# Head norms of a differential attention: repeating the inverse roots over all partitions through DRAM instead of by a copy and four transposes

## The chip, the cores and the metric

The kernel runs on one core of one Trainium2 chip. The core has five engines that work at the same time and meet through semaphores: TensorE (PE; its weight loads are shown apart as PEld), VectorE (DVE), ScalarE (ACT), GpSimd (POOL) and SyncE (SP). Sixteen DMA engines move data between DRAM and the on-chip memory SBUF; a transfer is issued by SyncE, ScalarE or GpSimd, each of which has its own queue and works through it in order. TensorE writes only to PSUM, a small memory of eight banks.

The metric is the time of one execution of the whole program on the device, in microseconds (us). Lower is better. A profile is taken in an execution of its own.

## The reference

One decoder layer over a sequence of 1024 positions with 1024 channels, all in float32: a token mixer with two branches (differential attention A with four heads, and a dilated window attention B with three groups of four heads), gates, an output projection, and then a gated MLP with a short convolution. The change concerns branch A alone:

```python
    oa = diff_attention(qa, ka, va, lam)              # (softmax1 - lam * softmax2) @ v, causal
    oa = rms_norm(oa, diff_head_g[l]) * (1.0 - lam_init)
    ya = oa.reshape(b, s, A_WIDTH) @ w_a_out[l]

def rms_norm(x, g):
    xf = x.astype(jnp.float32)
    y = xf * lax.rsqrt(jnp.mean(xf * xf, axis=-1, keepdims=True) + NORM_EPS)
    return (y * g.astype(jnp.float32)).astype(x.dtype)
```

Every position of every head has 128 output values. They are divided by the root of their mean square. This is the head norm: one inverse root for each position and head.

## The kernel before, in words

All products keep float32 accuracy by splitting each operand into a high and a low part (`split`, line 148) and adding three TensorE products (`mm3`, line 153). The program goes through stages: norms and values at the start, attention A, attention B, gates and output projections, then the MLP.

**Attention A.** Head after head (loop at line 915), the kernel works on eight query blocks of 128 positions in the order 6, 7, 4, 5, 2, 3, 0, 1 (`attend_a`, line 749). For a block it computes two score rows (lines 767 and 768, into one of two `s` PSUM banks), adds the mask and takes the maxima on VectorE (line 770), exponentiates on ScalarE (line 777), combines both softmaxes (line 784), transposes the result through a `pt` PSUM bank (`turned`, line 693; two `pt` banks) and multiplies by the values (`pv`, line 703). The output `osb` lies transposed: the 128 channels of the head on the partitions, 512 positions along the free dimension. Projections of the next head, of the first heads of attention B and of gates fill TensorE's time between the blocks (`proj_t`, line 235, with `rotated`, line 679, or `put_gate`, line 248, as evacuation; three `acc` PSUM banks). Their weights are loaded by SyncE (line 126) and split by ScalarE and VectorE (lines 149 and 146).

**The head norm.** `head_norm` (line 829) runs once for each half of 512 positions of each of the four heads, so eight times. ScalarE squares `osb` into a tile with the tag `hn` (line 832), which has one buffer. Then two steps are put off:

- `sums` (line 836): products with a column of ones, one for each block of 128 positions (line 840; the trace holds eight TensorE instructions for the four), add the squares over the 128 channels. The result has the positions of a block on the partitions, four columns for four blocks. `rsqrt` (line 159) makes the inverse root from them in twelve small VectorE instructions on 128x4 values (lines 166 to 179). Then a VectorE copy (line 843) repeats each of the four columns 128 times into `spread`, a 128x512 tile in the `hn` buffer.
- `norm` (line 845): four TensorE transposes (line 848) turn `spread` in blocks into a `pt` bank. Now every partition holds the inverse roots of all 512 positions along the free dimension. VectorE multiplies `osb` by this bank (line 849), and SyncE stores the result to `oa_d` in DRAM (line 850).

**What sets the order.** `later(n, fn)` (line 266) puts a step off by n query blocks: `sums` is due after one, `norm` after three. The steps that are due are called between the blocks, at a raised priority. From the instructions called in this way a planner makes each engine's queue: it simulates a timeline with costs of its own for every instruction and transfer, and issues what is ready by priority. So the order on an engine follows from the priorities and from when the planner expects an operand. Once written, a queue is worked through in order: an instruction that waits holds up everything behind it on its engine.

**GpSimd.** `side` (line 724) is `nc.gpsimd.dma_start`, a transfer issued by GpSimd. In the stretch of attention A its queue holds only the masks: `mask_a` before it (line 719), and `mask_b` for attention B at its end (lines 939 to 946), whose place in SBUF becomes free when an `osb` has been stored. In attention B `merge` (line 1042) uses the queue: it reads the statistics from `st_d` (line 1048), stores its weights to `e_d` (line 1071) and reads them back repeated on all partitions into `mw` (line 1077).

Of the kernel before, what the change touches and what calls it, by code (L numbers as in the profile page):

```python
# [15 lines left out]
F32 = mybir.dt.float32  # L16
# [3 lines left out]
ALU = mybir.AluOpType  # L20
# [4 lines left out]
P = 128  # L25
S = 1024
D = 1024
KC = D // P
AH, QK = 4, 64
# [58 lines left out]
def trunk(ctx: ExitStack, tc: tile.TileContext, a, out):  # L88
    nc = tc.nc
    dma = nc.sync.dma_start  # L90

    def open_pool(stack, name, bufs=1, side="left", **kw):
        if "space" not in kw:
            kw.update(side=side, reuse_waits="tile")
        return stack.enter_context(tc.tile_pool(name=name, bufs=bufs, **kw))
# [3 lines left out]
    cols, gpre, rstd = (edge[:, i * 8 : (i + 1) * 8] for i in range(3))  # L99
# [3 lines left out]
    dram = open_pool(ctx, "dram", space=DRAM)  # L103
    acc = open_pool(ctx, "acc", bufs=3, space=PSUM)
    pt = open_pool(ctx, "pt", bufs=2, space=PSUM)

    def psum(dt=F32, pool=acc, tag="acc"):
        return pool.tile([P, 512], dt, tag=tag, name=tag)
# [50 lines left out]
    def rsqrt(ss, n, pool, tag, eps=EPS):  # L159

        width = ss.shape[-1]
        v, y, w = (pool.tile([P, width], F32, tag=tag + c, name=tag + c) for c in "vyw")
        if isinstance(eps, float):
            nc.vector.tensor_scalar(v, ss, 1.0 / n, eps, op0=ALU.mult, op1=ALU.add)
        else:
            nc.vector.scalar_tensor_tensor(v, ss, 1.0 / n, eps, op0=ALU.mult, op1=ALU.add)
        nc.vector.tensor_scalar(y.bitcast(I32), v.bitcast(I32), -0.5, RSQRT_MAGIC, op0=ALU.mult, op1=ALU.add)

        f = 1.0
        for _ in range(3):  # L170
            if width == 1:
                nc.vector.tensor_scalar(w, y, y, v, op0=ALU.mult, op1=ALU.mult)
                nc.vector.tensor_scalar(y, w, -3.0 * f * f, y, op0=ALU.add, op1=ALU.mult)
            else:
                nc.vector.tensor_tensor(w, y, y, op=ALU.mult)
                nc.vector.tensor_tensor(w, w, v, op=ALU.mult)
                nc.vector.scalar_tensor_tensor(y, w, -3.0 * f * f, y, op0=ALU.add, op1=ALU.mult)
            f = -2.0 * f * f * f
        nc.vector.tensor_scalar(y, y, 1.0 / f, None, op0=ALU.mult)
        return y  # L180

    def rsqrt_row(x, y):

        v, r, w = (tiny.tile([P, 1], F32, tag="r1" + c, name="r1" + c) for c in "vyw")
        if y is None:
            nc.vector.tensor_scalar(v, x, EPS * D, None, op0=ALU.add)
        else:
            nc.vector.tensor_scalar(v, x, y, EPS * D, op0=ALU.add, op1=ALU.add)
        nc.scalar.activation(r, v, AF.Sqrt, scale=1.0 / D)
        nc.vector.reciprocal(r, r)  # L190

        nc.vector.tensor_scalar(w, r, r, v, op0=ALU.mult, op1=ALU.mult)
        nc.vector.tensor_scalar(w, w, -3.0 * D, r, op0=ALU.add, op1=ALU.mult)
        return w
# [9 lines left out]
    ident = const.tile([P, P], F32, name="ident")  # L204
# [10 lines left out]
    ob_d = dram.tile([BH, P, S], F32, name="ob_d")  # L215
    og_d = dram.tile([BH, BG, P, S], F32, name="og_d")
    st_d = dram.tile([BH, BG, 2, S], F32, name="st_d")
    e_d = dram.tile([BH, BG, S], F32, name="e_d")
    v_d = dram.tile([S, 2048], F32, name="v_d")
    gt_d = dram.tile([2 * KC, P, S], F32, name="gt_d")  # L220
# [45 lines left out]
    def later(n, fn, ahead=30):  # L266

        due.append((clock[0] + n, fn, ahead))
        due.sort(key=lambda d: d[0])
# [175 lines left out]
    with ExitStack() as st_y:  # L445
# [170 lines left out]
        for n in range(8, len(steps_v)):  # L616
            p, i, k = steps_v[n]
# [24 lines left out]
            if k == 0 and (p, i) in places_y:  # L642
                q, name, pool = places_y[p, i]
# [73 lines left out]
    wk_a = open_pool(st_a, "work_a", side="right")  # L717
# [6 lines left out]
    side = nc.gpsimd.dma_start  # L724
# [104 lines left out]
    def head_norm(h, half, osb, eps4):  # L829

        sq = wk_a.tile([P, 512], F32, tag="hn", name="sq", bufs=1)
        nc.scalar.activation(sq, osb, AF.Square)
        cols = slice(half * 512, (half + 1) * 512)
        spread = []

        def sums():
            ps = psum(F32, ps_o, "o")
            for b in range(4):
                c, o = slice(b * P, (b + 1) * P), ps[:, b : b + 1]
                nc.tensor.matmul(o, sq[:, c], ones[:, 0:1], start=True, stop=True)  # L840
            r = rsqrt(ps[:, :4], P, tiny, "rh", eps4)
            spread.append(wk_a.tile([P, 4, P], F32, tag="hn", name="spread", bufs=1))
            nc.vector.tensor_copy(spread[0], r.unsqueeze(2).to_broadcast([P, 4, P]))

        def norm():
            rr = psum(F32, pt, "pt")
            for b in range(4):
                nc.tensor.transpose(rr[:, b * P : (b + 1) * P], spread[0][:, b], ident)
            nc.vector.tensor_tensor(osb, rr, osb, op=ALU.mult)
            dma(oa_d[h][:, cols], osb)  # L850

        later(1, sums)
        later(3, norm)
# [285 lines left out]
    pair, g, h = steps[-1]  # L1139
# [76 lines left out]
    with st2:  # L1216
# [50 lines left out]
        for m in range(8):  # L1267
# [3 lines left out]
            hn = res.tile([P, D], F32, tag="hn", name="hn", bufs=3)  # L1271
# [13 lines left out]
            r = rsqrt_row(sm[:, 0:1], sm[:, 1:2])  # L1285
# [394 lines left out]
    for m in range(4):  # L1680
# [8 lines left out]
        r = rsqrt_row(sums[m][:, 0:1], sums[m][:, 1:2])  # L1689
# [55 lines left out]
```

## Time and profile before

| what | value |
|---|---|
| time, median of 3 runs | 1694.68 us (1693.86 to 1694.88) |
| the profiled execution's own time | 1692.04 us |
| its span, from the first to the last instruction | 1690.3 us |
| mean granted TensorE clock | 0.997 |
| TensorE busy | 1671.6 us, 99% of the span |
| VectorE busy | 1360.1 us, 80% |
| ScalarE busy | 892.2 us, 53% |
| GpSimd busy | 106.7 us, 6% |
| mean DMA rate | 128 GB/s |

The page of a profile has numbered parts. Part 1 gives each engine's busy time, its share of the span and its instructions. Part 2 cuts the span into 40 equal slices of 42.3 us and shows the busy share of each in tenths (9 is 90% or more). Other views group instructions by line (count, then shortest, median and longest duration in ns, then first and last start in us), show them in order of time (start in us, duration in us, engine, line, operation, output and inputs, count; in brackets the idle time of the engine before it and what ended that time), add up waits (total us, times, longest us), or give the busy time of every engine in a window. For transfers there is the time from issue to landing. Matmuls are pipelined: their durations overlap, so the distance between two starts tells how long one holds the array.

The eight head norms lie between about 277 and 546 us from the span's start. The first multiply of line 849 starts at 292.6 us, the last at 544.9 us.

### The profile page before, as it was taken

The numbers are of one execution on the slowest core, as the hardware profiler recorded it, in microseconds if no ns is written. First come the engines' busy times: TensorE is split into PE (matmuls) and PEld (weight loads), VectorE is DVE, ScalarE is ACT, GpSimd is POOL, SyncE is SP. The second block draws the span as 40 slices with busy tenths as digits, with TensorE's granted clock in tenths as the row PEclk, the third lists the DMA queues.
The fourth block names the chain that finished last, engine by engine and source line by source line (L and its number), as shares of the span: only waits on it lengthen the run. The fifth ranks groups of instructions, "written<-read, shape, count | busy, mean of one in ns | idle before, by whom it ended". The sixth has DMA issues, their size and how long they took to land. (4 is left out here: it accounts for less than half of the span.)

```text
span 1690.3 us, 22665 instructions
## 1 busy us (share of the span) xinstructions
PE 1671.6 (99%) x7890; PEld 1396.2 (83%) x7890; DVE 1360.1 (80%) x2509; ACT 892.2 (53%) x1663; POOL 106.7 (6%) x174
## 2 busy tenths in 40 slices
PE   9999999999999999999999999999999999999997
PEld 7888888888888888888888888888888888888885
DVE  8794686877777787788766865999999999699967
ACT  7643575655554777667554532454444444255453
POOL 0031000000000000010123400300000000000000
PEclk9999999999999999999999999999999999999998
DMA  8777311214112122343676531122222222396524
GB/s 274 227 270 221 99 59 62 88 57 119 51 63 81 53 74 77 107 128 111 208 267 221 187 112 63 38 106 94 94 81 87 90 79 87 112 339 213 184 75 162
DMA packets 104451, 216.41 MB, mean 128 GB/s; under 512 B 12992, under 2 KB 22144, under 8 KB 104336
## 3 DMA queue, kind: packets, MB, share of 16 engines
q1 hardware_dynamic: 89296, 171.28, 30.6%
q0 software_dynamic: 10288, 35.28, 6.3%
q10 hardware_dynamic: 4752, 8.39, 1.3%
q8 instruction: 62, 1.02, 0.2%
q14 instruction: 53, 0.43, 0.1%
HBM read 167.05 MB, written 47.86 MB: 127 GB/s over the span
## 5 line engine op out<-in xcount | busy, mean ns | idle before, releaser
L157 PE MATMUL acc<-xl,whi 128*128 128x512 f32 x768 | 303.0, 394 | 0.0
L155 PE MATMUL acc<-xh,whi 128*128 128x512 f32 x768 | 301.8, 393 | 0.0
L156 PE MATMUL acc<-xh,wlo 128*128 128x512 f32 x768 | 301.7, 393 | 0.0
L149 ACT ACTIVATE whi<-raw 128x512 fp32r<-128x512 f32 (+1 forms) x252 | 155.9, 626 | 176.5 <-PE acc L157 90.6
L146 DVE TENSOR_TENSOR wlo<-raw,whi 128x512 fp32r<-128x512 f32 (+1 forms) x252 | 178.8, 716 | 34.3 <-ACT whi L149 30.1
L156 PEld LDWEIGHTS acc<-xh,wlo 128*128 128x128 f32 x768 | 144.4, 188 | 28.1
L157 PEld LDWEIGHTS acc<-xl,whi 128*128 128x128 f32 x768 | 144.4, 188 | 28.0
L155 PEld LDWEIGHTS acc<-xh,whi 128*128 128x128 f32 x768 | 144.4, 188 | 27.5
L155 PE MATMUL acc<-mh,whi 128*128 128x512 f32 x400 | 155.8, 390 | 0.3 <-ACT mh L149 0.3
L156 PE MATMUL acc<-mh,wlo 128*128 128x512 f32 x400 | 155.6, 389 | 0.0
L157 PE MATMUL acc<-ml,whi 128*128 128x512 f32 x400 | 155.3, 389 | 0.0
L684 ACT ACTIVATE t<-acc 64x512 f32<-64x512 f32 (+1 forms) x160 | 94.6, 591 | 59.0 <-PE acc L157 57.1
L1456 DVE TENSOR_TENSOR u<-acc,u 128x512 f32<-128x512 f32 x133 | 91.1, 689 | 21.3 <-PE acc L157 21.1
L149 ACT ACTIVATE whi<-s 128x512 fp32r<-128x512 f32 x76 | 46.9, 627 | 101.1 <-PE acc L157 86.8
L685 DVE TENSOR_TENSOR t<-acc,cos 128x512 f32<-128x512 f32 x64 | 44.2, 691 | 58.3 <-ACT t L684 57.7
L155 PEld LDWEIGHTS acc<-mh,whi 128*128 128x128 f32 x400 | 75.1, 188 | 15.9 <-ACT mh L149 0.5
L157 PEld LDWEIGHTS acc<-ml,whi 128*128 128x128 f32 x400 | 75.1, 188 | 15.7
L156 PEld LDWEIGHTS acc<-mh,wlo 128*128 128x128 f32 x400 | 75.1, 188 | 15.6
L1580 PE MATMUL acc<-whi,wlo 128*128 128x512 f32 x220 | 77.5, 389 | 0.0
L1579 PE MATMUL acc<-whi 128*128 128x512 f32 x220 | 76.4, 389 | 0.0
L1581 PE MATMUL acc<-wlo,whi 128*128 128x512 f32 x220 | 73.1, 389 | 0.0
L777 ACT ACTIVATE s<-s,mx 128x896 f32<-128x896 f32 (+7 forms) x64 | 49.3, 771 | 35.2 <-DVE mx L770 18.9
(389 smaller groups left out, 3933.2 us busy)
## 6 DMA issues: line engine op xcount, KB each, us to landing
raw<-in_w_in SPq DMA_DIRECT2D x96, 256.0 KB, 2.9
raw<-in_w_up SPq DMA_DIRECT2D x88, 256.0 KB, 2.7
raw<-in_w_v SPq DMA_DIRECT2D x71, 256.0 KB, 4.5
raw<-c_d SPq DMA_DIRECT2D x48, 256.0 KB, 3.5
c_d<-c SPq DMA_DIRECT2D x22, 512.0 KB, 2.7
raw<-in_w_down SPq DMA_DIRECT2D x37, 256.0 KB, 3.7
v_d<-yv POOLq DMA_DIRECT2D x32, 256.0 KB, 4.2
gt_d<-gate ACTq DMA_DIRECT2D x32, 256.0 KB, 2.1
```

The lines of the kernel that those rows point to most:

```text
L146: eng.tensor_tensor(lo, src, hi.bitcast(F32), op=ALU.subtract)
L149: copy = nc.scalar.activation(hi, src, AF.Copy)
L155: nc.tensor.matmul(o, sh, mh, start=first, stop=False, skip_group_check=on)
L156: nc.tensor.matmul(o, sl, mh, start=False, stop=False, skip_group_check=on)
L157: nc.tensor.matmul(o, sh, ml, start=False, stop=last, skip_group_check=on)
L684: nc.scalar.activation(t1[dst], ps[src], AF.Copy)
L685: nc.vector.tensor_tensor(t2, ps, cos[:, sl], op=ALU.mult)
L777: exp = nc.scalar.activation(sc[c][:, :w], sc[c][:, :w], AF.Exp, bias=mx[:, c, 0:1], scale=-1.0, accum_out=den[:, c : c + 1])
L1456: nc.vector.tensor_tensor(to, made(p), x, op=ALU.add)
L1579: nc.tensor.matmul(banks[m], gh[:, tk], wh, start=f == 0, stop=False)
L1580: nc.tensor.matmul(banks[m], gl[:, tk], wh, start=False, stop=False)
L1581: nc.tensor.matmul(banks[m], gh[:, tk], wl, start=False, stop=f == NH - 1)
```

## The change

The inverse roots `r` (128 positions on the partitions, four columns) go to DRAM into a new tensor `rn_d`, in the order of the positions, and come back repeated on all 128 partitions. Both transfers are issued by GpSimd, in `sums`. The second one waits for the first. The copy and the four transposes are gone, and the multiply takes the roots from SBUF and not from PSUM. `spread` keeps its size, tag and buffer.

```diff
@@ -215,6 +215,7 @@
     st_d = dram.tile([BH, BG, 2, S], F32, name="st_d")
+    rn_d = dram.tile([AH, S], F32, name="rn_d")
     e_d = dram.tile([BH, BG, S], F32, name="e_d")
@@ -839,14 +840,12 @@
                 c, o = slice(b * P, (b + 1) * P), ps[:, b : b + 1]
                 nc.tensor.matmul(o, sq[:, c], ones[:, 0:1], start=True, stop=True)
             r = rsqrt(ps[:, :4], P, tiny, "rh", eps4)
-            spread.append(wk_a.tile([P, 4, P], F32, tag="hn", name="spread", bufs=1))
-            nc.vector.tensor_copy(spread[0], r.unsqueeze(2).to_broadcast([P, 4, P]))
+            side(rn_d[h, cols].rearrange("(b p) -> p b", p=P), r)
+            spread.append(wk_a.tile([P, 512], F32, tag="hn", name="spread", bufs=1))
+            side(spread[0], rn_d[h, cols].partition_broadcast(P))
 
         def norm():
-            rr = psum(F32, pt, "pt")
-            for b in range(4):
-                nc.tensor.transpose(rr[:, b * P : (b + 1) * P], spread[0][:, b], ident)
-            nc.vector.tensor_tensor(osb, rr, osb, op=ALU.mult)
+            nc.vector.tensor_tensor(osb, spread[0], osb, op=ALU.mult)
             dma(oa_d[h][:, cols], osb)
 
         later(1, sums)
```

## The prediction

> **What bounds the kernel now.** I read the page's first two parts first, then the table of windows for the stretch that holds all eight head norms (240 to 560 us).
>
> ```profile
> span 1690.3 us, 22665 instructions
> PE 1671.6 (99%) x7890; PEld 1396.2 (83%) x7890; DVE 1360.1 (80%) x2509; ACT 892.2 (53%) x1663; POOL 106.7 (6%) x174
> PE   9999999999999999999999999999999999999997
> DMA  8777311214112122343676531122222222396524
> ...
> core 0: us, PE busy (x) PEld busy (x) DVE busy (x) ACT busy (x) POOL busy (x), PEclk, DMA share, GB/s
> 240.00:560.00 320.00, 320.00 (x1618) 270.44 (x1617) 239.76 (x630) 176.16 (x376) 1.48 (x4) 1.00 0.23 74
> ```
>
> TensorE (PE) never pauses in that stretch: 320.00 busy of 320.00 us, at full granted clock. VectorE (DVE) is busy for 239.76 us, 75%; GpSimd (POOL) does next to nothing; the DMA engines are 23% busy, and the DMA digits for these slices (the sixth to the fourteenth) are lower than in the later stage that reads through DRAM (digits 3 to 7). So a TensorE instruction taken away here shortens the stretch, and a VectorE instruction taken away does so only if TensorE was about to wait for it. The nearest waits of TensorE lie behind the stretch; they come from ScalarE and VectorE work of the second attention, not from a head norm:
>
> ```profile
> 572.72 0.66 PE L697 MATMUL pt<-ident,bs 128*128 128x128 f32 x4 [1.35 <-ACT rows L1034]
> 576.79 0.33 PE L157 MATMUL s<-kl,qh 128*128 128x128 f32 x1 [1.36 <-DVE kl L879]
> ```
>
> **What is removed.** There are eight head norms (four heads, two halves). Each loses four transposes (L848), one widening copy (L843) and one use of a `pt` PSUM bank. The multiply (L849) stays and reads SBUF instead of PSUM. Groups by line, then TensorE's timeline at the first norm:
>
> ```profile
> L848 PE MATMUL pt<-ident,spread x32: 270/272/274, 292.0 to 544.6; 128*128 128x128 f32 x32
> L843 DVE COPY spread<-rhy x8: 417/424/427, 287.8 to 539.3; 128x512 f32<-128x512 f32 x8
> L849 DVE TENSOR_TENSOR osb<-pt,osb x8: 683/691/692, 292.6 to 544.9; 128x512 f32<-128x512 f32 x8
> ...
> 291.76 0.40 PE L156 MATMUL acc<-xh,wlo 128*128 128x512 f32 x1
> 292.00 0.60 PE L848 MATMUL pt<-ident,spread 128*128 128x128 f32 x4
> 292.44 0.49 PE L697 MATMUL pt<-ident,s 128*128 128x128 f32 x3
> ```
>
> The 272 ns of one transpose are latency, for they overlap. What counts is the distance between starts: from 292.00 to 292.44, four transposes hold the array for 0.44 us. 8 x 0.44 = **3.5 us** of TensorE time. That is the whole gain on the engine that sets the end. The eight copies free 8 x 0.424 = 3.4 us of VectorE, which I cost at nothing: TensorE does not wait for VectorE here. Were that cover gone, they would be worth up to another 3.4 us. The multiply keeps its 0.69 us; both inputs in SBUF are nothing new (from below and above: between 0.69 and, if PSUM were what slows it, the copy's 0.42 us, so at most 8 x 0.27 = 2.2 us of VectorE, also covered). I take zero. The freed `pt` bank can only help the transposes of the scores, which do not wait now; zero.
>
> **What is added.** Per norm, GpSimd issues a store of the 128x4 roots (512 pieces of 4 bytes) and, when that has landed, a read of one 2 KB row by all 128 partitions (256 KB). Neither is in the trace, but the second attention's merge does the same to its weights: store `e_d` (384 pieces of 32 bytes), then broadcast `mw`.
>
> ```profile
> 717.07 0.32 DVE L1070 TENSOR_TENSOR me<-me,mm 128x8 f32<-128x8 f32 x3
> ...
> 717.95 0.77 POOL L1071 DMA_DIRECT2D e_d<-me  x1 [35.51 <-ACT t L684]
> 721.83 1.63 POOL L1077 DMA_DIRECT2D mw<-e_d  x3 [3.12 <-DMA e_d<-me]
> ...
> L1071 POOL DMA_DIRECT2D e_d<-me x4: 755/772/776, 717.9 to 886.3; - x4
> DMA to landing us min/median/max: 2.1/3.2/3.8
> ...
> L1077 POOL DMA_DIRECT2D mw<-e_d x24: 537/542/583, 721.8 to 901.6; - x24
> DMA to landing us min/median/max: 3.4/4.2/8.3
> ...
> mr<-st_d POOLq DMA_DIRECT2D x4, 24.0 KB, 2.6
> ```
>
> Operand ready at 717.39, store issued at 717.95: 0.6 us. The store lands after 3.2 us (2.1 to 3.8). From its landing to the next issue, 721.83 - 717.95 - 3.2 = 0.7 us. The read lands after 4.2 us (3.4 to 8.3; these are three in a row, and here it is one). Sum: 0.6 + 3.2 + 0.7 + 4.2 = **8.7 us**, between 0.6 + 2.1 + 0.7 + 3.4 = 6.8 and 0.6 + 3.8 + 0.7 + 8.3 = 13.4. I take the middle: DMA engines are emptier here, but 4-byte pieces are unknown. More pieces alone are no price in these rows: `mr` moves 768 of them (24 KB in 32 bytes) and lands in 2.6 us. Issuing costs GpSimd 0.77 + 0.54 us per norm, on an engine busy for 1.48 us in the stretch.
>
> [...]
>
> **When the roots are due.** From the last step of the root to the multiply, at the first norm, the tightest and the loosest:
>
> ```profile
> 285.69 0.17 DVE L179 TENSOR_SCALAR rhy<-rhy 128x4 f32<-128x4 f32 x1
> 292.64 0.69 DVE L849 TENSOR_TENSOR osb<-pt,osb 128x512 f32<-128x512 f32 x1 [0.20 <-PE pt L848]
> ...
> 326.25 0.17 DVE L179 TENSOR_SCALAR rhy<-rhy 128x4 f32<-128x4 f32 x1
> 331.08 0.69 DVE L849 TENSOR_TENSOR osb<-pt,osb 128x512 f32<-128x512 f32 x1 [0.94 <-PE pt L848]
> ...
> 401.90 0.16 DVE L179 TENSOR_SCALAR rhy<-rhy 128x4 f32<-128x4 f32 x1
> 409.58 0.69 DVE L849 TENSOR_TENSOR osb<-pt,osb 128x512 f32<-128x512 f32 x1 [2.11 <-PE pt L848]
> ```
>
> Gaps of 6.8, 4.7 and 7.5 us; I use 6.1, the middle of the ends. If the planner leaves the multiply where it is, it is 8.7 - 6.1 = 2.6 us late, and VectorE stands still with everything queued behind it: score maxima (L770), rotations (L685), splits (L146). Does TensorE feel it? Behind the norm at 447.48:
>
> ```profile
> 448.08 0.68 DVE L770 CUSTOM_DVE_ANT_0 s<-s,mask_a 128x512 f32<-128x512 f32 x1
> ...
> 447.00 0.47 PE L767 MATMUL s<-k,q 128*128 128x512 f32 x1
> ...
> 453.35 0.40 PE L767 MATMUL s<-k,q 128*128 128x512 f32 x1
> ```
>
> Scores have two banks. The maximum at 448.08 frees one at 448.76, and TensorE writes it again only at 453.35 (the scores of 447.00 are in the other): 4.6 us of cover. So 2.6 us late costs TensorE nothing, and VectorE's 25% of idle time takes it up. Without this cover it would cost 8 x 2.6 = 21 us.
>
> The store to `oa_d` on SyncE's queue (L850) also slides by 2.6 us, and the weight loads behind it:
>
> ```profile
> SPq L850 <- DVE osb L849: 26.2, 6, 8.0
> ...
> ACT whi L149 <- PE acc L157: 20.3, 17, 2.3
> ACT whi L149 <- DMA raw<-in_w_in: 1.4, 1, 1.4
> ...
> 523.98 0.31 POOL L939 MEMSET mask_b<- 128x256 f32 x1 [359.41 <-DMA oa_d<-osb]
> ...
> L976 DVE CUSTOM_DVE_ANT_0 bs<-s,mask_b x25: 274/419/435, 549.6 to 600.0; 128x256 f32<-128x256 f32 x18, 128x128 f32<-128x128 f32 x7
> ```
>
> That queue already stands up to 8.0 us before such a store, and the weights' splits wait 17 times for TensorE and once for a load: zero. On GpSimd's queue, which waits for each store to land, only the mask of the second attention stands behind the new transfers; it is written at 523.98 and read from 549.6: 25 us of cover, zero.
>
> **Sum.** -3.5 us. The profiled execution took 1692.04 us, its span 1690.3 and 1.74 around it; it would become 1688.5. It lies 2.6 us under the median of the runs, 1694.68; against that median I forecast **1691.2 us**.
>
> **The rivals.** (1) *The gain is not passed on.* The planner writes all queues anew from the changed program, and TensorE gets small waits elsewhere, or the 3.5 us run into a wait that is there. The two waits after the stretch, 1.4 us each, show the size: 1.5 to 3 us given back, 1693 to 1694. For it: the roots' lateness uses up half of the 4.6 us cover. Against it: no wait at all in the 320 us.
>
> (2) *Slower: the round trip outlasts the cover.* The place is the multiply on VectorE; the point from which it decides is 6.1 + 4.6 + 0.44 = 11.1 us from root to landing, where TensorE loses what it gained. At the upper bound, 13.4 us, it stalls 13.4 - 10.7 = 2.7 us, eight times 21.6, less 3.5: 1712.8. For it: reads that took 8.3 us, and pieces of 4 bytes. Against it: those reads fell among heavy transfers, which this stretch lacks. At 11.7 us, 1 us of stall per norm, it would be 1694.68 + 8 - 3.5 = 1699.2.
>
> [...]
>
> (3) *More than counted.* The new order also loses the two waits at 572 and 576: 1691.2 - 2.7 = 1688.5. For it: the shift moves the very work that meets there. Against it: nothing links them to the norms.
>
> **How the numbers follow.** Forecast 0.48, rival 1 0.20, rival 2 0.16 (from the point where it decides upwards), rival 3 0.16. A measurement of this kernel tells about 0.2% from no change, 3.4 us, that is 1691.3 or 1698.1. The forecast lies on that bound: I count 0.26 of its 0.48 as faster and 0.22 as the same. Faster 0.26 + 0.16 = 0.42; slower: rival 2 reaches 1698.1 only beyond 11.6 us, 0.14; same 0.22 + 0.20 + 0.02 = 0.44. The range goes from 1688.0, just under rival 3, to 1699.2, the one-microsecond case of rival 2, whose upper half stays out. Cases of both signs don't hold most of the chance; the forecast's own range is 1690 to 1692.5.
>
> **What would show it.** TensorE: 7858 matmuls, no L848, still 320 of 320 us in the stretch. VectorE: L843 gone, and waits of 1 to 4 us at L849 for the transfer of `spread`, 10 to 25 us in all, if the planner leaves the multiply in place; none if it moves it. The store should land in 2 to 4 us, the read in 3.4 to 5; more than 11 us from root to landing, or waits of TensorE for L770 or L685 between 240 and 560 us, would prove rival 2. The forecast is wrong if TensorE's busy time in the stretch falls below its length, or if its waits after 560 us grow by more than 2 us.

## The result, and the profile after

The changed kernel takes 1744.28 us (median of four runs, 1743.31 to 1746.36) against 1694.27 us before (1691.93 to 1694.88): 1.0298 times as long, with an interval of 1.0286 to 1.031. It is 50 us slower. Forecast were 1691.2 us, and at most 1699.2.

Parts 1, 2 and 4 of the page of the changed kernel; its profiled execution took 1744.85 us:

```profile
span 1743.1 us, 22636 instructions
PE 1687.3 (97%) x7858; PEld 1407.1 (81%) x7858; DVE 1352.7 (78%) x2501; ACT 890.7 (51%) x1663; POOL 119.5 (7%) x190
PE   9999999898899799999999999999999999999997
PEclk9999999899899899999999999999999999999999
...
PE 74%; issue 12%; DMA 7%; DVE 5%; ACT 2%; SPq 0%; POOL 0%; DVEq 0%; POOLq 0%; ACTq 0%
```

TensorE (PE) has the forecast 32 instructions fewer, 7858, and yet it is busy for 15.7 us longer (1687.3 against 1671.6). It also idles more: 1743.1 - 1687.3 = 55.8 us of the span, against 1690.3 - 1671.6 = 18.7, so 37.1 us more. Together 15.7 + 37.1 = 52.8 us, which is the whole difference of the spans. So there are two things to explain: new waits, and TensorE instructions that became slower. The two digit rows show them in the same places: PE falls below 9 in the eighth, tenth, eleventh and fourteenth slice, and PEclk, the granted clock, in the eighth, eleventh and fourteenth.

The windows of the changed kernel: first the stretch of 320 us that TensorE filled before, then five pieces around the norm whose root is ready at 327 us (columns: window, its length, then for each engine the busy us and instructions, then clock, DMA share and rate).

```profile
core 0: us, PE busy (x) PEld busy (x) DVE busy (x) ACT busy (x) POOL busy (x), PEclk, DMA share, GB/s
240.00:560.00 320.00, 293.29 (x1420) 245.89 (x1419) 211.72 (x566) 156.90 (x337) 8.62 (x13) 0.95 0.26 73
...
325.00:336.50 11.50, 11.46 (x58) 9.30 (x56) 6.61 (x19) 4.49 (x10) 0.77 (x1) 1.00 0.58 62
336.50:343.30 6.80, 0.00 (x0) 0.00 (x0) 1.34 (x3) 0.00 (x0) 0.54 (x1) 0.82 0.28 74
343.30:347.70 4.40, 4.39 (x15) 4.11 (x16) 2.04 (x7) 1.97 (x6) 0.00 (x0) 0.50 0.32 119
347.70:380.00 32.30, 32.30 (x167) 27.31 (x166) 21.59 (x65) 15.34 (x40) 0.51 (x1) 1.00 0.17 58
```

TensorE is idle for 320.00 - 293.29 = 26.7 us of the stretch that it filled before. At this norm it stands still for 6.8 us; then it works for 4.4 us at a granted clock of 0.50 and needs nearly the full 4.4 us for 15 instructions; only after 347.7 has it the full clock back.

What it waited for is shown by the timelines of VectorE, GpSimd and TensorE at that norm (start, duration, instruction, and in brackets the idle time before it and what ended that time):

```profile
326.95 0.16 DVE L179 TENSOR_SCALAR rhy<-rhy 128x4 f32<-128x4 f32 x1
...
341.96 0.69 DVE L848 TENSOR_TENSOR osb<-spread,osb 128x512 f32<-128x512 f32 x1 [10.23 <-DMA spread<-rn_d]
342.57 1.15 DVE L146 TENSOR_TENSOR pt<-pt 128x512 fp32r<-128x512 f32 x2
...
327.60 0.77 POOL L843 DMA_DIRECT2D rn_d<-rhy  x1 [29.31 <-DVE rhy L179]
338.42 0.54 POOL L845 DMA_DIRECT2D spread<-rn_d  x1 [10.06 <-DMA rn_d<-rhy]
...
336.07 0.39 PE L156 MATMUL acc<-xh,wlo 128*128 128x512 f32 x1
343.31 0.80 PE L710 MATMUL o<-pt,vh 128*128 128x512 f32 x1 [6.85 <-DVE pt L146]
```

The last step of the root starts at 326.95; the multiply at 341.96, 15.0 us later. VectorE stood for 10.23 us of that time with the split of `pt` (L146) queued behind the multiply, and TensorE, whose last product before it starts at 336.07, then stood for 6.85 us for that split. The groups by line and the waits of VectorE and TensorE say the same of all eight norms:

```profile
L843 POOL DMA_DIRECT2D rn_d<-rhy x8: 757/767/780, 286.2 to 583.5; - x8
DMA to landing us min/median/max: 8.5/9.6/10.6
...
L845 POOL DMA_DIRECT2D spread<-rn_d x8: 542/542/558, 297.7 to 593.7; - x8
DMA to landing us min/median/max: 3.5/3.7/4.1
...
DVE osb L848 <- DMA spread<-rn_d: 78.2, 8, 11.8
...
PE o L710 <- DVE pt L146: 15.3, 3, 8.0
PE pt L698 <- DVE s L785: 8.0, 2, 4.7
PE s L155 <- DVE stat L975: 6.7, 1, 6.7
...
PE s L768 <- DVE mx L771: 3.4, 1, 3.4
```

The read lands in 3.7 us, as forecast. The store takes 9.6 us where the forecast had 3.2 and at most 3.8. VectorE waits 9.8 us on average at the eight multiplies (78.2 us in all), and TensorE for the work behind them.

### The profile page after: what moved, and what is told of

It reads as the page before. It is cut to its first block, busy times and chain, and to the rows that moved or that the text cites. A ratio compares the mean times of both kernels' runs of the same rounds, so it can differ in the third digit from the quotient of the medians.

```text
span 1743.1 us, 22636 instructions
## 1 busy us (share of the span) xinstructions
PE 1687.3 (97%) x7858; PEld 1407.1 (81%) x7858; DVE 1352.7 (78%) x2501; ACT 890.7 (51%) x1663; POOL 119.5 (7%) x190
## 4 chain that ended last, share of the span: by engine, by line
PE 74%; issue 12%; DMA 7%; DVE 5%; ACT 2%; SPq 0%; POOL 0%; DVEq 0%; POOLq 0%; ACTq 0%
PE acc L155 16%; PE acc L157 16%; PE acc L156 16%; DMA rn_d<-rhy 3%; PE acc L1579 3%; PE acc L1578 3%; PE acc L1580 3%; PE acc L1259 2%; PE acc L1257 2%; PE acc L1258 2%; DMA spread<-rn_d 1%; PE o L710 1%; PE pt L698 1%; PE s L157 1%; PE s L156 1%
## 5 line engine op out<-in xcount | busy, mean ns | idle before, releaser
L156 PE MATMUL acc<-xh,wlo 128*128 128x512 f32 x768 | 305.7, 398 | 0.0
L146 DVE TENSOR_TENSOR wlo<-raw,whi 128x512 fp32r<-128x512 f32 (+1 forms) x252 | 176.3, 706 | 38.2 <-ACT whi L149 36.1
L710 PE MATMUL o<-pt,vh 128*128 128x512 f32 (+1 forms) x188 | 56.3, 366 | 19.0 <-DVE pt L146 15.3
```

Source lines behind the costliest of these rows:

```text
L146: eng.tensor_tensor(lo, src, hi.bitcast(F32), op=ALU.subtract)
L156: nc.tensor.matmul(o, sl, mh, start=False, stop=False, skip_group_check=on)
L710: nc.tensor.matmul(o[:, :, q0 : q1 + 1], vs[b // 4][0][:, b % 4, c], t, start=first and n == 0, stop=False)
```

## The experiments

Three questions were open. Is it the store's price that makes the loss, or the two transfers as such (their queue, their traffic), or a new order of the engines' queues? What in the store is dear? And is there anything left to gain?

**One: pieces of 16 bytes instead of 4.** The roots of a partition lie side by side in DRAM (128 pieces, not 512), and the multiply reads them in steps of four. The order of the instructions is that of the changed kernel on every engine.

```diff
-            side(rn_d[h, cols].rearrange("(b p) -> p b", p=P), r)
+            side(rn_d[h, cols].rearrange("(p b) -> p b", b=4), r)
...
-            nc.vector.tensor_tensor(osb, spread[0], osb, op=ALU.mult)
+            o4, r4 = (t.rearrange(f, b=4) for t, f in ((osb, "c (b p) -> c b p"), (spread[0], "c (p b) -> c b p")))
+            nc.vector.tensor_tensor(o4, r4, o4, op=ALU.mult)
```

> One change to the changed kernel: the four roots of a partition are stored side by side (128 pieces of 16 bytes instead of 512 of 4), and the multiply reads the repeated roots in steps of four, so that the result is the same. Theory A (price of the pieces): the 8.5 to 10.6 us from issue to landing come from the pieces of 4 bytes; the store now lands in 2 to 4 us like the store of e_d, VectorE waits for the repeated roots some 78 - 8 x 6.5 = 26 us in all instead of 78, TensorE's cover of some 5 us per norm holds, there is no half clock between 280 and 620 us, and the time is 1691 us (1689 to 1694). Theory B (price of the path): any store by GpSimd's queue lands this late here, because VectorE's work or the many transfers hold it up; it still lands after 8 us or more and the time stays at 1735 to 1745. Theory C (order): the planner's new order made TensorE's waits; the order of VectorE is the same in both kernels, so the time stays above 1730 whatever the store takes.

Measured: 1692.54 us against 1693.19 for the kernel before, 0.999 (0.9981 to 1.0). Of the 50 us nothing is left. Part 1 of this kernel's page, the landing of its store, VectorE's wait and the group of its multiply:

```profile
PE 1671.3 (99%) x7858; PEld 1395.0 (83%) x7858; DVE 1358.0 (80%) x2501; ACT 890.8 (53%) x1663; POOL 117.9 (7%) x190
...
DMA to landing us min/median/max: 1.7/1.8/2.5
...
DVE osb L849 <- DMA spread<-rn_d: 19.6, 7, 4.1
...
L849 DVE TENSOR_TENSOR osb<-spread,osb x8: 1061/1069/1077, 293.6 to 547.1; 128x512 f32<-128x512 f32 x8
```

The store lands in 1.8 us, and VectorE's waits fall from 78.2 to 19.6 us, at most 4.1 at once. With the same two transfers on the same queue and the same order of work, the form of the store makes the loss; theories B and C are out. The other difference, the reading in steps of four, works the other way: it costs the multiply 1.07 us instead of 0.69.

That no gain is left has a reason of its own. TensorE's timeline and windows of this kernel, at the second attention:

```profile
570.77 0.66 PE L698 MATMUL pt<-ident,bs 128*128 128x128 f32 x4 [1.59 <-ACT rows L1034]
574.84 0.33 PE L157 MATMUL s<-kl,qh 128*128 128x128 f32 x1 [1.35 <-DVE kl L879]
...
573.50:581.00 7.50, 6.14 (x24) 5.02 (x25) 7.50 (x15) 4.97 (x12) 0.00 (x0) 0.77 0.18 71
853.00:861.00 8.00, 5.96 (x23) 4.65 (x22) 3.32 (x6) 5.61 (x8) 0.85 (x1) 0.79 0.92 349
```

The two waits are those of before, but here half clock follows (a mean of 0.77 over 7.5 us), where the expectation had none before 620 us, and again at 853 us behind a wait of 2.0 us (0.79 over 8.0 us; a product of 512 columns starts 0.43 us after the one before it at 857 to 859 us, 0.23 at 852 and from 860 us). By these means each place lacks 1.7 us of full clock (0.23 x 7.5 and 0.21 x 8.0), 3.4 us together, and TensorE's busy time is no smaller than before (1671.3 against 1671.6). That alone uses up the 3.5 us that the transposes gave, and the wait of 2.0 us comes on top.

**Two: the multiply on GpSimd, the store of the change.** The late operand then holds up GpSimd's queue and not VectorE's.

```diff
-            nc.vector.tensor_tensor(osb, spread[0], osb, op=ALU.mult)
+            nc.gpsimd.tensor_tensor(osb, spread[0], osb, op=ALU.mult)
```

> One change to the changed kernel: GpSimd does the multiply by the repeated roots, not VectorE. The store keeps its pieces of 4 bytes. Theory A (the late multiply held up VectorE, and VectorE held up TensorE): the store still lands in 8.5 to 10.6 us, but nothing of VectorE's stands behind it, so TensorE's waits of 3 to 8 us at each norm vanish; one wait of up to 6 us may remain at the start of the second attention, whose mask is behind the last multiply on GpSimd's queue: 1691 to 1700 us. Theory B (path) makes the same forecast here. Theory C (order, or the transfers' traffic): TensorE goes on waiting between 280 and 600 us, 1720 us or more.

Measured: 1708.45 us, 1.0091 (1.0077 to 1.0105). The store still takes 9.8 us. 36 of the 50 us are gone, so most of the loss came by way of VectorE's queue; but the time misses the expected range by 8 us. Waits and groups of this kernel show two more ways, of which the expectation had the second:

```profile
ACT sq L833 <- POOL osb L848: 21.1, 4, 7.7
DVE bs L975 <- POOL mask_b L941: 10.6, 1, 10.6
...
L848 POOL TENSOR_TENSOR osb<-spread,osb x8: 1256/1291/2067, 302.4 to 562.3; 128x512 f32<-128x512 f32 x8
```

The next norm's squares need the one `hn` buffer in which `spread` lies, and so wait for the late multiply; and the mask of attention B, behind the last norm on GpSimd's queue, comes 10.6 us late. They cost TensorE waits of 3.3 us (three together) and 5.6 us, and the mean granted clock is 0.993 (before 0.997).

**Three: the two transfers beside the old way.** The kernel before, with the same store and a shorter read that nothing uses.

```diff
             r = rsqrt(ps[:, :4], P, tiny, "rh", eps4)
+            side(rn_d[h, cols].rearrange("(b p) -> p b", p=P), r)
+            aside = wk_a.tile([P, 64], F32, tag="aside", name="aside", bufs=1)
+            side(aside, rn_d[h, cols][:64].partition_broadcast(P))
```

> The kernel before, with its copy and its four transposes, and beside them the store of the roots in pieces of 4 bytes and a read of 64 of them on all partitions into a tile that nobody uses. Theory A: the store lands in 8.5 to 10.6 us as in the changed kernel, nobody waits for it but GpSimd's queue, and the time is that of the kernel before, 1694.3 us, within 3 us. If the transfers themselves disturb (traffic, descriptors, the planner): 1700 us or more.

Measured: 1695.6 us against 1693.19, 1.0011 (1.0002 to 1.002). The window and the landing of the store in this kernel:

```profile
240.00:560.00 320.00, 320.00 (x1622) 270.64 (x1621) 240.84 (x630) 174.12 (x368) 11.61 (x20) 1.00 0.28 75
...
DMA to landing us min/median/max: 9.7/10.8/11.3
```

The store is as slow (10.8 us) with nobody waiting for it, and TensorE works for 320.00 of 320.00 us. So the price belongs to the store, not to what the change moved around it, and these transfers as such harm nothing in this stretch: only the waiting for them does. (The read here is an eighth of the real one; experiment one has it in full.)

**Four: the transposes gone, nothing in their place.** The kernel before without the turning (each position is multiplied by the root of another; the turning is left out).

```diff
-            rr = psum(F32, pt, "pt")
-            for b in range(4):
-                nc.tensor.transpose(rr[:, b * P : (b + 1) * P], spread[0][:, b], ident)
+            rr = spread[0].rearrange("p b q -> p (b q)")
```

> The kernel before without the four transposes and without any transfer: the multiply takes the tile that the copy fills, so each position is multiplied by a root of another position; the turning is what is left out. It prices the one gain of the prediction by itself. Term of 3.5 us right: 1694.3 - 3.5 = 1690.8 us (1689.5 to 1692). If removing TensorE instructions here is worth nothing, 1694; if the planner's new order makes waits of its own, above 1696.

Measured: 1687.98 us, 0.9964 (0.9952 to 0.9977), so 5.2 us less. Part 1 of its page:

```profile
PE 1667.9 (99%) x7858; PEld 1392.1 (83%) x7858; DVE 1360.7 (81%) x2509; ACT 891.5 (53%) x1663; POOL 106.3 (6%) x174
```

TensorE's busy time falls by 1671.6 - 1667.9 = 3.7 us: the forecast term was 3.5. Where the rest of the 5.2 us comes from isn't shown. The two waits at 572 and 576 us, 2.7 us together, are gone in this order of work, but gaps of 0.9 to 1.4 us at 8 us and between 855 and 866 us came in exchange, and all of TensorE's idle time in the span fell only from 18.7 to 1686.0 - 1667.9 = 18.1 us. To take the transposes out is thus worth 4 to 8 us by the interval, of which 3.7 have a known place.

**Five: pieces of 8 bytes, 256 of them.** A value between one and the change.

```diff
-            side(rn_d[h, cols].rearrange("(b p) -> p b", p=P), r)
+            side(rn_d[h, cols].rearrange("(c p b) -> p c b", c=2, b=2), r.rearrange("p (c b) -> p c b", c=2))
...
+            o4 = osb.rearrange("m (c b p) -> m c b p", c=2, b=2)
+            r4 = spread[0].rearrange("m (c p b) -> m c b p", c=2, b=2)
+            nc.vector.tensor_tensor(o4, r4, o4, op=ALU.mult)
```

> The changed kernel with the store in 256 pieces of 8 bytes, two roots side by side, and the multiply reading the repeated roots in the matching order; VectorE's order is that of the changed kernel. It gives a third point between 512 pieces of 4 bytes (9.6 us to landing) and 128 of 16 bytes (1.8 us). Price by the number of pieces: 256 / 512 of 9.6, so 4 to 5 us; VectorE is then some 4.5 us late per norm, about what TensorE's cover takes, and the time is 1693 to 1705 us. Price of the 4-byte size alone: the store lands in 2 to 3 us and the time is that of the 16-byte kernel, 1692.5 us.

Measured: 1702.13 us against 1694.0, 1.0054 (1.004 to 1.0068). Landing and wait in this kernel:

```profile
DMA to landing us min/median/max: 3.3/3.7/5.3
...
DVE osb L850 <- DMA spread<-rn_d: 35.1, 8, 6.8
```

A store of 3.7 us lies between the 4 to 5 us of the price by number and the 2 to 3 us of the price by size, so it decides for neither. It is about what the prediction had as its upper bound (3.8), and it already costs 8 us. The three kernels have one order of work through all eight norms (this one differs from 600 us on) and make a row: a store of 1.8, 3.7 and 9.6 us gives VectorE waits of 19.6, 35.1 and 78.2 us and a time of 1692.5, 1702.1 and 1744.3 us.

**Six: what is dear in the store.** The kernel before with stores that nobody waits for, another form for each head: 512 adjacent pieces of 4 bytes; 512 pieces of 4 bytes that begin 64 bytes apart; 512 adjacent pieces of 16 bytes; and the first form from SyncE.

```diff
+            if h == 0:
+                side(ra_d[0, cols].rearrange("(b p) -> p b", p=P), r)
+            if h == 1:
+                side(rb_d[cols, 0:1].rearrange("(b p) c -> p (b c)", p=P), r)
+            if h == 2:
...
+                side(rc_d[cols].rearrange("(b p) c -> p b c", p=P), four)
+            if h == 3:
+                dma(ra_d[3, cols].rearrange("(b p) -> p b", p=P), r)
```

> The kernel before with stores that nobody waits for, two of each kind, one kind for each head: head 0, 512 adjacent pieces of 4 bytes from GpSimd's queue; head 1, 512 pieces of 4 bytes that lie 64 bytes apart in DRAM; head 2, 512 adjacent pieces of 16 bytes (each root four times); head 3, 512 adjacent pieces of 4 bytes from SyncE's queue. If the number of pieces sets the price, all of GpSimd's land in 8 to 11 us. If it is the size, head 2 lands in 2 to 4 us. If neighbours of 4 bytes hinder each other in DRAM, head 1 lands in 2 to 4 us. If it is GpSimd's making of the descriptors, head 3 lands in 2 to 4 us. The time stays within 3 us of the kernel before, 1694 us.

Measured (one execution, 1695.2 us), the transfers of this kernel with KB and the us to landing:

```profile
ra_d<-rhy POOLq DMA_DIRECT2D x2, 2.0 KB, 10.0
rb_d<-rhy POOLq DMA_DIRECT2D x2, 2.0 KB, 2.6
rc_d<-four POOLq DMA_DIRECT2D x2, 8.0 KB, 2.3
ra_d<-rhy SPq DMA_DIRECT2D x2, 2.0 KB, 11.3
```

The same 512 pieces of 4 bytes land in 2.6 us when they don't touch, and 512 that touch in 2.3 us when they have 16 bytes. So it is neither the number of pieces nor their 4 bytes alone, and not GpSimd's queue (11.3 us from SyncE): it is pieces of 4 bytes written side by side (10.0 us). Nor is it the moment of the store: in the changed kernel all eight of the first form, spread over 300 us, take 8.5 to 10.6 us.

**Seven and eight: 16 bytes, and the multiply on GpSimd.** What each had alone (one and two), put together; in eight the last head's two multiplies stay on VectorE, so that the mask of attention B isn't behind them.

```diff
-            nc.vector.tensor_tensor(osb, spread[0], osb, op=ALU.mult)
+            o4, r4 = (t.rearrange(f, b=4) for t, f in ((osb, "c (b p) -> c b p"), (spread[0], "c (p b) -> c b p")))
+            nc.gpsimd.tensor_tensor(o4, r4, o4, op=ALU.mult)
```

and in eight:

```diff
+            (nc.vector if h == AH - 1 else nc.gpsimd).tensor_tensor(o4, r4, o4, op=ALU.mult)
```

> The 16-byte store and the multiply on GpSimd together. No wait of VectorE for the roots, 8 x 1.07 us of VectorE freed; TensorE's 3.5 us come through if no half clock arises: 1689 to 1691 us. If the mask of the second attention, behind the last multiply on GpSimd's queue, or the next square, which waits for the buffer of the roots, becomes late, there is a wait of TensorE of 1 to 4 us at 300 to 560 us and the time is 1693 to 1697 us. If the order of the queues alone decides, anything in between.

> As the run before, but in the last head VectorE multiplies, so that the mask of the second attention comes about 2 us earlier. If the mask's wait is what costs there, this one is 1 to 4 us faster than the run before; otherwise the two are alike.

Measured: 1690.96 us, 0.9985 (0.9976 to 0.9994), and 1690.38 us, 0.9983 (0.9974 to 0.9992), against 1694.0. Both are ahead of the kernel before by 3 to 4 us, and eight has the lowest time of the kernels of the study that compute all of the reference, though seven can't be told from it. Part 1 of eight's page:

```profile
PE 1669.0 (99%) x7858; PEld 1394.1 (83%) x7858; DVE 1357.8 (80%) x2495; ACT 890.8 (53%) x1663; POOL 125.2 (7%) x196
```

TensorE's busy time is 1671.6 - 1669.0 = 2.6 us down, 1669.0 in seven too. Why it is not the 3.7 us of experiment four was not shown; the mean granted clock is 0.997 in both, as before. The two times don't differ, so with a store this short (1.8 us in both) the mask's place costs nothing.

**Nine: the price by distance.** The kernel before with 512 pieces of 4 bytes that begin 8, 16 and 32 bytes apart, and 64 from SyncE.

```diff
+    apart_d = [dram.tile([S, w], F32, name=f"apart{w}_d") for w in (2, 4, 8, 16)]
...
+            to = apart_d[h][cols, 0:1].rearrange("(b p) c -> p (b c)", p=P)
+            (dma if h == 3 else side)(to, r)
```

> The kernel before with stores of 512 pieces of 4 bytes that nobody waits for, whose distance in DRAM grows from head to head: 8 bytes (head 0), 16 bytes (head 1), 32 bytes (head 2), all from GpSimd's queue, and 64 bytes from SyncE's queue (head 3). If neighbours within 64 bytes hinder each other in proportion to their number, against 10 us for adjacent ones: about 5, 3.5, 3 and 2.3 us. If any distance between pieces is enough, all land in 2 to 3 us. If SyncE's queue has a price of its own for such pieces, head 3 stays near 11 us. The time stays within 3 us of the kernel before.

Measured (one execution, 1695.44 us), the groups of this kernel head by head:

```profile
L844 POOL DMA_DIRECT2D apart_d<-rhy x2: 767/774/780, 286.3 to 326.8; - x2
DMA to landing us min/median/max: 4.9/5.2/5.5
...
DMA to landing us min/median/max: 2.5/3.1/3.6
...
DMA to landing us min/median/max: 2.2/2.3/2.4
...
DMA to landing us min/median/max: 2.1/2.1/2.1
```

From 10.0 us side by side (experiment six) the price falls to 5.2, 3.1, 2.3 and 2.1 us at 8, 16, 32 and 64 bytes. It falls about as the first of the three forecasts has it, and at 32 bytes and more it is gone. That the number of pieces in one short stretch of DRAM sets it would fit, but was not tried by itself.

## Why the prediction was wrong

**The step that failed is the store's 3.2 us.** It was taken from `e_d`, the nearest row, and both of its bounds (2.1 and 3.8) came from that row too. But `e_d` and `mr` move pieces of 32 bytes, and `mr` is a read. "More pieces alone are no price in these rows" was right, and experiment six bears it out: 512 pieces land in 2.3 to 2.6 us if they don't lie side by side as 4 bytes. What no row of before held is the piece's size together with its neighbours. The text named the 4-byte pieces as unknown and then gave the unknown no bound beyond the known row's. The measured 9.6 us (8.5 to 10.6) is two and a half times that bound. Even for pieces of 32 bytes 3.8 us was tight: another store of such pieces in the trace before, `st_d` from `stat` (L1023, from SyncE's queue, in the second attention), took 4.2 us and up to 7.1.

In pieces of 16 bytes the same roots land in 1.8 us (experiment one), and 512 pieces of 4 bytes that begin 64 bytes apart in 2.1 to 2.6 us (experiments nine and six). Why 4 bytes side by side are dear, no run here shows.

**The rest of the chain held.** 0.5 us from root to store (forecast 0.6), 0.6 to 0.9 from its landing to the read (0.7), and 3.7 us of reading (4.2). With the measured store and read the sum is 0.6 + 9.6 + 0.7 + 3.7 = 14.6 us; from the end of the root to the multiply the eight norms took 13.7 to 15.6 us, 14.4 on average.

**The cover was sized right on average, and it was used up.** Forecast: TensorE has 4.6 us before it feels VectorE's lateness. VectorE waited 78.2 us, and TensorE's new waits behind the eight multiplies (26.7 us in the window, and about 9.3 at 571 and 594 us) add up to 36.0: (78.2 - 36.0) / 8 = 5.3 us per norm. But it differs from norm to norm: at 439 us VectorE waited 10.8 us and TensorE 8.0, which leaves 2.8 us of cover, at 571 us 9.9 and 2.7, which leaves 7.2. And the score banks, from which the 4.6 us were taken, ran out first at one norm only (L768, 3.4 us). Elsewhere TensorE waited for the split of `pt` (L146, three waits, 15.3 us), for the combined softmax (L785, two, 8.0 us), and behind the last two norms for a square and for the statistics of attention B (2.7 and 6.7 us).

**Rival 2 had the mechanism, not the size.** Its place (the multiply on VectorE) was right; it ended at 13.4 us and 1712.8. By its own working a chain of 14.4 us gives 1694.68 + 8 x (14.4 - 10.7) - 3.5 = 1720.8. The measured time is 23.5 us more. Its point (11.1 us) lay too far out: in experiment five the eight chains take 8.2 to 10.6 us, and yet TensorE waits 2.3 and 2.4 us at two norms, where the cover is 3.7 and 2.6 us, and the mean granted clock of that kernel is 0.994 (before 0.997). (A wait of 3.4 us at 863 us, far behind the norms, adds to the 8 us of that kernel.)

**Most of that remainder is a term that nobody had: the half clock.** Behind the waits TensorE's granted clock is 0.50 in nine stretches of 3.4, 6.8 or 10.2 us, 51.2 us in all (the first at 303.3 us, the last at 907.5); before the change it had none between 6 and 1681 us. At half clock a product of 512 columns starts 0.43 us after the one before it (at 445 us), at full clock 0.23 us (at 447 us). By the clock's 0.50 the 51.2 us do the work of 25.6, so up to 25.6 us are lost: an estimate. TensorE's busy time shows what is really lost: it rose by 15.7 us while 3.5 us of instructions went, so 19.2 us. That agrees with the clock: TensorE was busy for 38.3 of the 51.2 us, and half of that is 19.1. The waits themselves are the smaller part of the remainder, 36.0 us where the working above has 8 x 3.7 = 29.6. The prediction costed a wait of TensorE at its length only.

In each of TensorE's seven waits of 3.3 us and more (3.36 to 7.98 us) the clock falls to 0.50, 2.1 to 4.6 us after the wait begins. The other two of the nine stretches stand behind shorter waits: 2.65 us at 571 us, and 1.59 and 1.35 us at 620 and 624 us.

**The gain was right.** The term of 3.5 us measured 3.7 as busy time (experiment four), and the 1687.98 us there lie near rival 3 (the waits at 572 and 576 go too, 1688.5). That is partly luck, for the two waits did go, but other gaps took their place; and it wasn't the changed kernel. What the widening copy is worth was not tried by itself.

**The mask was placed wrongly.** "25 us of cover, zero" took the mask's time from before. It lies behind the last two transfers on GpSimd's queue. The timelines of GpSimd, VectorE and TensorE in the changed kernel:

```profile
594.25 0.33 POOL L938 MEMSET mask_b<- 128x256 f32 x1
...
594.90 0.28 POOL L941 TENSOR_SCALAR_AFFINE_SELECT mask_b<-mask_b 128x128 f32<-128x128 f32 x1
...
597.30 0.69 DVE L848 TENSOR_TENSOR osb<-spread,osb 128x512 f32<-128x512 f32 x1 [11.78 <-DMA spread<-rn_d]
...
600.32 0.28 DVE L975 CUSTOM_DVE_ANT_0 bs<-s,mask_b 128x128 f32<-128x128 f32 x1
...
601.01 0.58 PE L155 MATMUL s<-kh,qh 128*128 128x256 f32 x1 [6.67 <-DVE stat L975]
```

The mask is begun at 594.2 us, 70 us later than before (523.98), because the last norm's store and read stand ahead of it. Even so it has no share of the loss here: it is ready at 595.2 us, and its first reader (L975) starts only at 600.32, because it stands on VectorE's queue behind the last multiply, which waited 11.78 us for its roots. TensorE's wait of 6.7 us at 594 us (for `stat`, L975) belongs to that multiply. In experiment two, where VectorE doesn't wait for the roots, the same mask did cost TensorE 5.6 us.

**The waits of the multiply.** "Waits of 1 to 4 us, 10 to 25 us in all" describes experiment one (19.6 us, at most 4.1), whose store lands a little faster than forecast (1.8 us, not 2 to 4), and not the change. The planner left the multiply about where it was, 4 to 14 instructions behind the root's last step (6 to 13 before), and so gave nothing back.

## What to carry to other kernels

When a transfer in the trace is to price a new one, compare the size of the pieces and their spacing in DRAM, not the bytes and the count: 2 KB as 512 adjacent values of 4 bytes took 9.6 us to land, as 128 runs of 16 bytes 1.8, and the reader of the data can undo the order by its access pattern (here for 0.38 us per multiply in steps of four). A read was no price for the store here: `mr`, in pieces of 32 bytes, lands in 2.6 us, the store in 9.6. Where a bound is taken from a row that differs in the very thing called unknown, it is no bound. And the waits of several us on the engine that sets the end cost more than their length here: 37.1 us more of idle time brought 19.2 us of slow work behind it.

## What the runs showed of the hardware

- A store of 512 values of 4 bytes lands later the closer they lie in DRAM: 10.0 us side by side, then 5.2, 3.1, 2.3 and 2.1 to 2.6 us when they begin 8, 16, 32 and 64 bytes apart (experiments six and nine). From SyncE's queue it is about the same (11.3 side by side, 2.1 at 64 bytes). Why isn't shown.
- In the changed kernel's trace TensorE's granted clock is 0.50 in stretches of 3.41, 6.83 and 10.24 us, and the 18 changes of the clock between 303 and 911 us lie 3.413 us or a multiple of it apart (to 0.002 us). Half clock came with each of the seven waits of 3.3 us and more there, and also behind shorter ones: 2.65 us (the changed kernel, at 571 us), 1.59 and 1.35 us close together (the changed kernel at 620 and 624 us, experiment one at 570 to 577 us) and 2.0 us (experiment one, at 853 us). Before the change, 1.35 and 1.36 us at the same work brought none. What decides between them isn't shown.
- A VectorE product of two 128x512 float32 tiles took 0.69 us with both in order (the changed kernel, L848) and 1.07 us with one read in steps of four values (experiment one, L849); on GpSimd it took 1.29 us in order (experiment two, L848).
